# Expert weights in 2-MB tiles with 16-KB runs instead of 1-MB tiles with 8-KB runs

## The chip, the cores and the metric

The kernel runs on one core of a Trainium2 chip. The metric is the device time of one execution in microseconds (us). The engines are called as in the profile: PE (TensorE, matrix products; PEld its weight loads), DVE (VectorE), ACT (ScalarE), POOL (GpSimd) and SP (SyncE, which issues nearly all the DMAs here). One core has 16 DMA engines.

## The reference

Two layers of a diffusion backbone in float32, with 256 tokens of a latent stream and 256 tokens of context, 1024 channels each. Every layer has a front (modulation from a condition vector, layer norm, one wide projection, attention and a gated scan side by side, an output projection, layer norm) and then a mixture of 16 experts:

```python
def expert_choice_ffn(u, w_router, w_gate, w_up, w_down):
    cap = CAPACITY_FACTOR * n // N_EXPERTS            # 32 tokens for each expert
    aff = jax.nn.softmax(u @ w_router, axis=-1)
    top_w, top_idx = lax.top_k(jnp.swapaxes(aff, 1, 2), cap)
    xs = jax.vmap(lambda ub, ib: ub[ib])(u, top_idx)
    h = jax.nn.silu(einsum('becd,edf->becf', xs, w_gate)) * einsum('becd,edf->becf', xs, w_up)
    y = einsum('becf,efd->becd', h, w_down) * top_w[..., None]
    ...                                               # y is added at the chosen tokens

for l in range(2):
    mod = silu(c) @ w_mod[l] + b_mod[l]               # six vectors of 1024: shifts, scales, gates
    ...
    x = post_norm(ALPHA * x + g1 * y, ...)            # y from the token mixer
    u = layer_norm(x) * (1.0 + sc2) + sh2
    x = post_norm(ALPHA * x + g2 * expert_choice_ffn(u, ...), ...)
    ...                                               # layer 0 does the same for the context
```

Each of `w_gate`, `w_up` and `w_down` of an expert is 1024 by 1024 float32, 4 MB. The experts of both layers are 384 MB of the 526 MB that are moved.

## The kernel before, in words

The program is front 0, experts 0, front 1, experts 1. In layer 0 the latent and the context tokens go through the experts together (64 rows for each expert, `S = 2`, `G = 2`), in layer 1 only the latent tokens (32 rows, `S = 1`, `G = 4`). G is the number of column blocks that are computed side by side in PE, NW = 1024 / G is the width of a block and NB = NW / 128.

**The weights.** `moe` walks over the experts e0 to e15. For each, `eload` (L1023) reads gate, up and down as four tiles of 1 MB each. A tile holds 256 rows of the matrix; partition p takes two rows that follow one another in memory, so that a run is 8 KB. SP issues these DMAs at L1029, in the order of the program, through one queue. The last matrix of all, e15's down, is read by `eload_cols` as four tiles of 256 columns (runs of 1 KB), each by two DMAs of 512 KB.

**The slots.** A tile goes into the next slot of a list (`next(slots)`), and the DMA waits until PE has read what stood in that slot. The lists are written by hand at the end of `tile_kernel`, over the slots that `moe_pools` makes: layer 0 has 16 slots for good and two (`once`, tiles `wY` and `wg2 OH`) that serve one time, layer 1 has 19. The list of layer 1 starts with e0's gate in `s[13:17]` and, after 19 MB, comes back to `s[13]`. Since SP issues in order, a DMA that waits for its slot holds up all that are behind it.

**The order of rows.** As partition p holds rows 2p and 2p + 1, product k takes its 128 rows with a step of two: `pairs(v, k)` is the view with that step, and everything that meets the weights along their rows is cut in the same way: the gathered tokens (L1154), `h` before its transposes (L1251), the router weights `wraw` (two DMAs on POOL, L1052) and the modulation of section 6 and 8.

**Modulation.** `mod_steps` computes two of the twelve half-vectors of a layer at a time: it multiplies pieces of `w_mod` (L292), and at the end `mod_cols` (L243) turns the rows into columns by two transposes on PE (L248) and adds the bias on DVE. It does so for q0 = 0 to 10 in steps of two in each layer; q0 = 6 and 8 are the ones whose columns meet the weights.

**Experts on PE.** Gate and up are L1236 (`acc<-w,xs`), down is L1269 (`o<-w,hT`), the end of the last expert L1204 and L1212. A scheduler may move instructions of one engine past one another where data allow it; PE begins the gate of the next expert ahead of the down of this one. A float32 matmul is two records in the trace, a transpose one. Hence 1 MB of weights is 8 records in layer 0 and 16 in layer 1.

Of the kernel before, what the change touches and what calls it, by code (L numbers as in the profile page):

```python
# [19 lines left out]
D = 1024  # L20
# [71 lines left out]

def pairs(v, k):

    return v[:, 256 * (k // 2) + k % 2:256 * (k // 2) + 256:2]

# [11 lines left out]
def tile_kernel(ctx, tc, x, c, ctx_in, c_ctx, w_mod, b_mod, w_in, attn_sink, lb_fw, lb_bw, norm_g,  # L108
# [121 lines left out]
    nc.gpsimd.dma_start(brow, _dram(b_mod, 0, [[256, 48], [1, 256]]))  # L230
    pt = ob()
    for m in range(2):
        nc.tensor.transpose(pt[:, 48 * m:48 * m + 48], brow[:, 128 * m:128 * m + 128], ident[:48, :48])
        nc.tensor.transpose(pt[:, 96 + 48 * m:144 + 48 * m], brow[:, m:256:2], ident[:48, :48])
    for z, a, b in ((0, 0, 6), (1, 6, 10), (0, 10, 12)):
        for m in range(2):
            pv = pt[:, 96 * z + 48 * m:96 * z + 48 * m + 48].rearrange("p (l q j) -> p l q j", l=DEPTH, q=12)
            nc.vector.tensor_copy(BM[:, :, a:b, m::2], pv[:, :, a:b])
    for sec in (1, 4):
        v = BM[:, :, 2 * sec:2 * sec + 2]  # L240
        nc.vector.tensor_scalar(v, v, 1.0, None, op0=ALU.add)

    def mod_cols(l, pm, a, q0, dq, ns):  # L243

        nc.vector.tensor_copy(a, pm[:, 0:256])
        pt = mdb()
        for m in range(2):
            nc.tensor.transpose(pt[:, 128 * m:128 * m + 128], pairs(a, m) if q0 in (6, 8) else a[:, 128 * m:128 * m + 128], ident)  # L248
# [768 lines left out]
    def moe(l, X, M, slots):  # L1017
# [5 lines left out]
        def eload(src, e):  # L1023

            ts = []
            for h in range(4):
                w = next(slots)()
                w = w.rearrange("p (k n) -> p k n", k=2)
                in_order(loads, nc.sync.dma_start(w, _dram(src, (l * NE + e) * D * FF + 256 * h * FF, [[2 * FF, 128], [FF, 2], [1, FF]])))  # L1029
                ts.append(w)  # L1030
            return ts

        def eload_cols(src, e):

            ts = []
            for h in range(4):
                w = next(slots)().rearrange("p (k n) -> p k n", k=KT)
                for i in range(2):
                    in_order(loads, nc.sync.dma_start(w[:, i::2], _dram(src, (l * NE + e) * D * FF + i * FF + 256 * h,
                                                                        [[2 * FF, 128], [256 * FF, KT // 2], [1, 256]])))  # L1040
                ts.append(w)
            return ts

        def wrow(ts, k):
            return ts[k // 2][:, k % 2]

# [3 lines left out]
        nc.gpsimd.memset(wraw, 0.0)  # L1050
        for i in range(2):
            nc.gpsimd.dma_start(wraw[:, i::2, 0:NE], _dram(w_router, l * D * NE + i * NE, [[2 * NE, 128], [256 * NE, KT // 2], [1, NE]]))  # L1052

# [12 lines left out]
        def route(s):  # L1066
# [5 lines left out]
            for i in range(2):  # L1072
# [74 lines left out]
        def gather(gi, s, after=()):  # L1147

            for k4 in range(0, KT, 4):
                p = tr3() if gi else (ob, acc)[k4 // 4]()  # L1150
                for k in range(k4, k4 + 4):
                    for i in range(2):
                        t = 2 * s + i
                        ins = mm(p[:, 128 * (k - k4):128 * (k - k4) + 128], pairs(xh[:, t, :], k),  # L1154
                                 OHs[gi % 2][:, t].rearrange("p e c -> p (e c)"), start=(i == 0), stop=(i == 1))
                        if after:
                            in_order(list(after), ins)
# [68 lines left out]
        for gi in range(4):  # L1226
            for e4 in range(4):
# [38 lines left out]
                for kt in range(KT):  # L1266
                    j, m = kt // NB, kt % NB
                    for dj in range(G):
                        mm(py[MW * dj:MW * dj + MW, :NW], hT[:, 128 * m + MW * j:128 * m + MW * j + MW],  # L1269
                           wrow(wd, kt)[:, NW * dj:NW * dj + NW], start=(kt == 0), stop=(kt == KT - 1))  # L1270
                if e == 0:
# [70 lines left out]
    def moe_pools(l, st, S, zones, right=()):  # L1342

        M, slots, once = {}, [], []
        shapes = {"xh": [2 * S, D], "OH": [2 * S, 4, CAP], "xs": [KT, 4, 32 * S], "oT": [S, 256], **({"OH": [2, 4, CAP]} if S == 1 else {}), "pad": [1024]}
        rest = {"g2": [D], "OH": [2 * S, 4, CAP], "Y": [S, D]}
        parts = []
        for z, names in enumerate((right,) + zones if right else zones):
            Z = pool(sZ, f"ZR{l}", side="right") if names is right else pool(st, f"Z{l}{z}")
            for n in names:  # L1350
                if isinstance(n, int):
                    for i in range(n):

                        w = 2304 if z == 2 + (right != ()) else 2048
                        slots.append(lambda Z=Z, i=i, w=w: Z.tile([128, w], F32, name=f"w{i}", tag=f"w{i}")[:, :2048])
                elif n not in shapes:

                    once.append(lambda Z=Z, n=n: Z.tile([128, 2048], F32, name="w" + n, tag=n))
                    parts.append((n, lambda Z=Z, n=n: Z.tile([128, 2048], F32, name=n, tag=n)))
# [68 lines left out]
```

## Time and profile before

| | |
|---|---|
| median of 3 runs | 1807.12 us (1805.68 to 1808.17) |
| profiled execution, own time | 1810.56 us |
| its span in the profile | 1808.8 us |
| PE busy | 1552.1 us (86% of the span) |
| moved by DMA | 525.93 MB, mean 291 GB/s |
| experts 0, stretch in which DMA is full | about 567 to 960 us |
| experts 1, stretch in which DMA is full | about 1358 to 1777 us |

The own time of the profiled execution is 1.8 us above its span. [...] "x" is a count of records.

### The profile page before, as it was taken

How to read it: one execution, taken by the hardware profiler on the slowest of the kernel's cores; microseconds unless marked ns; L12 is line 12 of the kernel's file. 1: busy time of each engine (PE TensorE's matmuls, PEld its weight loads, DVE VectorE, ACT ScalarE, POOL GpSimd, SP SyncE). 2: the span in 40 equal slices, each digit the busy share in tenths (PEclk: the TensorE clock that was granted, in tenths of full speed). 3: DMA queues.
4: the chain of work that ended last, by engine and by line, in shares of the span. 5: the costliest groups of instructions: out<-in, count | busy, mean ns of one | idle time of the engine just before them, and what ended most of it. 6: DMA issues, size and time to landing. Idle time of an engine off the chain costs nothing.

```text
span 1808.8 us, 27428 instructions
## 1 busy us (share of the span) xinstructions
PE 1552.1 (86%) x11342; PEld 926.5 (51%) x11342; DVE 689.3 (38%) x1458; ACT 468.9 (26%) x884; POOL 296.9 (16%) x298
## 2 busy tenths in 40 slices
PE   6999998999979999898987999998968766766675
PEld 4777775788744433332223788775845322322222
DVE  4656666423651221211213756766751100100102
ACT  2437666423120100001001533676410000000000
POOL 2332222224300000000002633231610000000001
PEclk9999998999989999999999999998969777876877
DMA  9633224524679999999999753422689999999997
GB/s 319 199 105 118 82 71 151 197 85 146 264 301 381 421 421 421 421 422 421 421 422 363 235 159 112 146 94 85 243 337 413 420 421 421 420 421 421 421 421 289
DMA packets 159436, 525.93 MB, mean 291 GB/s; under 512 B 9896, under 2 KB 94064, under 8 KB 111184
## 3 DMA queue, kind: packets, MB, share of 16 engines
q1 hardware_dynamic: 157136, 517.33, 74.1%
q0 software_dynamic: 1456, 4.49, 0.7%
q10 hardware_dynamic: 720, 2.36, 0.4%
q8 instruction: 89, 1.46, 0.3%
q14 instruction: 35, 0.29, 0.0%
HBM read 523.10 MB, written 1.05 MB: 290 GB/s over the span
## 4 chain that ended last, share of the span: by engine, by line
PE 46%; DMA 43%; DVE 4%; ACT 2%; POOL 2%; issue 1%; SPq 1%; POOLq 0%; ACTq 0%; DVEq 0%
DMA w<-in_w_up_dram 14%; DMA w<-in_w_down_dram 14%; DMA w<-in_w_gate_dram 12%; PE acc L166 9%; PE acc L167 8%; PE acc L168 8%; PE acc L1236 5%; PE o L1269 2%; DMA wmod<-in_w_mod_dram 2%; PE md L292 2%; PE sc L740 1%; PE tr L735 1%; PE o L667 1%; PE hs L653 1%; PE sc L716 1%
## 5 line engine op out<-in xcount | busy, mean ns | idle before, releaser
L1236 PE MATMUL acc<-w,xs 128*32 128x256 f32 (+1 forms) x3064 | 406.6, 515 | 95.7 <-DMA w<-in_w_up_dram 51.1
L1236 PEld LDWEIGHTS acc<-w,xs 128*32 128x32 f32 (+1 forms) x3064 | 137.7, 130 | 345.9 <-issue 176.1
L1269 PE MATMUL o<-w,hT 128*32 128x256 f32 (+1 forms) x1432 | 189.3, 513 | 41.2 <-DMA w<-in_w_down_dram 26.8
L166 PE MATMUL acc<-uTh,wh 128*128 128x512 f32 (+1 forms) x592 | 213.1, 361 | 4.7 <-ACT sgs L858 3.6
L167 PE MATMUL acc<-uTl,wh 128*128 128x512 f32 (+1 forms) x592 | 210.2, 355 | 1.1 <-DVE uTl L396 1.1
L168 PE MATMUL acc<-uTh,wl 128*128 128x512 f32 (+1 forms) x592 | 210.1, 355 | 0.0
L1247 ACT ACTIVATE h<-acc 128x512 f32<-128x512 f32 (+1 forms) x32 | 15.7, 491 | 516.5 <-PE acc L1236 503.7
L477 POOL TENSOR_TENSOR wl<-win,wh 128x1024 fp32r<-128x1024 f32 x44 | 111.3, 2531 | 232.5 <-ACT wh L476 230.9
L1269 PEld LDWEIGHTS o<-w,hT 128*32 128x32 f32 (+1 forms) x1432 | 64.4, 132 | 145.5 <-issue 68.2
L1248 DVE TENSOR_TENSOR h<-h,acc 128x512 f32<-128x512 f32 (+1 forms) x32 | 17.7, 552 | 296.0 <-PE acc L1236 296.0
L166 PEld LDWEIGHTS acc<-uTh,wh 128*128 128x128 f32 x592 | 112.2, 190 | 28.7 <-issue 5.1
L167 PEld LDWEIGHTS acc<-uTl,wh 128*128 128x128 f32 x592 | 112.5, 190 | 17.6 <-DVE uTl L396 1.9
L168 PEld LDWEIGHTS acc<-uTh,wl 128*128 128x128 f32 x592 | 112.4, 190 | 15.7 <-issue 1.8
L476 ACT CAST wh<-win 128x1024 fp32r<-128x1024 f32 x84 | 83.9, 1047 | 80.5 <-PE acc L167 48.5
L1128 POOL TENSOR_TENSOR OW<-OH,aff 128x256 f32<-128x256 f32 x8 | 4.9, 617 | 584.5 <-PE sc L1251 569.6
L1292 DVE TENSOR_TENSOR Y<-o,g2 OH 32x512 f32<-32x512 f32 x60 | 41.2, 687 | 137.9 <-PE o L1269 137.1
L477 DVE TENSOR_TENSOR wl<-win,wh 128x1024 fp32r<-128x1024 f32 x40 | 55.5, 1389 | 80.4 <-ACT wh L476 80.4
L1253 ACT COPY hT<-sc 128x512 f32<-128x512 f32 (+1 forms) x32 | 15.3, 479 | 249.0 <-PE sc L1251 248.9
L1292 DVE TENSOR_TENSOR Y g<-o,Y g 32x256 f32<-32x256 f32 x60 | 25.2, 420 | 121.5 <-PE o L1269 120.8
L292 PE MATMUL md<-wmod,scol 128*32 128x256 f32 x640 | 58.0, 422 | 8.0 <-DMA wmod<-in_w_mod_dram 5.3
L562 DVE TENSOR_TENSOR K<-K,F 128x512 f32<-128x512 f32 x56 | 48.1, 859 | 11.0 <-PE hs L634 9.3
L331 POOL TENSOR_TENSOR mv<-mv,nhalf 128x1 f32<-128x1 f32 x26 | 24.4, 941 | 125.8 <-DVE mv L330 125.8
(453 smaller groups left out, 2393.9 us busy)
## 6 DMA issues: line engine op xcount, KB each, us to landing
w<-in_w_gate_dram SPq DMA_DIRECT2D x128, 1024.0 KB, 19.8
w<-in_w_up_dram SPq DMA_DIRECT2D x127, 1024.0 KB, 19.8
w<-in_w_down_dram SPq DMA_DIRECT2D x119, 1024.0 KB, 19.8
wmod<-in_w_mod_dram SPq DMA_DIRECT2D x80, 512.0 KB, 4.6
win<-in_w_in_dram SPq DMA_DIRECT2D x26, 1024.0 KB, 6.2
win<-in_w_in_dram SPq DMA_DIRECT2D x32, 512.0 KB, 5.2
wmod<-in_w_mod_dram SPq DMA_DIRECT2D x32, 256.0 KB, 6.3
wo<-in_w_out_dram SPq DMA_DIRECT2D x8, 1024.0 KB, 5.3
```

The costliest lines, as they stand in the source:

```text
L166: mm(p, a.hi, b.hi, start=start, stop=False, **kw)
L167: mm(p, a.hi, b.lo, start=False, stop=False, **kw)
L168: mm(p, a.lo, b.hi, start=False, stop=stop, **kw)
L292: mm(pm[32 * j:32 * j + 32, 0:256], scol[:, k, :], w[:, 256 * j:256 * j + 256], start=(k == 0), stop=(k == KT - 1))
L331: pows.append(nc.gpsimd.tensor_tensor(mv[:, 2:3], mv[:, 2:3], nhalf[:, 0:1], op=ALU.pow))
L476: nc.scalar.copy(hi[:, r], w[:, r])
L477: ins = eng.tensor_sub(lo[:, r], w[:, r], hi[:, r])
L562: nc.vector.tensor_tensor(kv, kv, _view(f, 0, [[nf + 1, 2], [2, nf // 2], [0, m]]), op=ALU.mult)
L653: mm(p[:, 256 * i:256 * i + 256], K[:, d, 256 + 128 * i:384 + 128 * i], Q[:, d, 0:256], start=(d == 0), stop=(d == 1), skip_group_check=True)
L1236: ins = mm(p[MW * j:MW * j + MW, :NW], xs[:, k, e4, :], wrow(w, k)[:, NW * j:NW * j + NW], start=(k == 0), stop=(k == KT - 1))
L1269: mm(py[MW * dj:MW * dj + MW, :NW], hT[:, 128 * m + MW * j:128 * m + MW * j + MW], wrow(wd, kt)[:, NW * dj:NW * dj + NW], start=(kt == 0), ...
L1292: nc.vector.tensor_tensor(o, py[r:r + 32, :NW], g2[r:r + 32, NW * dj:NW * dj + NW], op=ALU.mult)
```

## The change

The 16 (and 19) MB for weights are cut into 2-MB slots `d` where two neighbours can be taken, 6 in layer 0 and 7 in layer 1, and the slots `s` of 1 MB that are left. A tile in a `d` slot has 512 rows, four consecutive ones on each partition, runs of 16 KB. Where the list says `two`, the same 512 rows go into two 1-MB slots, with runs of 8 KB. Of the 96 steps of 2 MB that a layer takes from its list, 72 are `d` in layer 0 and 71 in layer 1. All that meets the rows is cut with a step of four (`quads`); in layer 1 `h` has two blocks of 128 columns (NB = 2), and so that its transposes still meet the rows, `share` gives gate and up a moving operand of two neighbouring elements in every four. Two transposes in `mod_cols` become eight small products for q0 = 6 and 8 (`fourths`), also once for `b_mod` at the start. The router weights are four DMAs on POOL instead of two, and e15's down four of 256 KB for each MB.

```diff
+    def fourths(o, v, n):
+        for m in range(4):
+            for j in range(2):
+                mm(o[64 * j:64 * j + 64, n * m:n * m + n], v[:, m:256:4], ident[:n, :n], start=True, stop=True, skip_group_check=True)
...
         pt = mdb()
+        if q0 in (6, 8):
+            fourths(pt, a, 128)
...
+                    nc.vector.tensor_tensor(MT[l][r, q0:q0 + 2, :, s], pv[r, :, j, :, s], BM[r, l, q0:q0 + 2, :], op=ALU.add)
+            return
...
         def eload(src, e):
-            for h in range(4):
-                w = next(slots)()
-                w = w.rearrange("p (k n) -> p k n", k=2)
-                in_order(loads, nc.sync.dma_start(w, _dram(src, (l * NE + e) * D * FF + 256 * h * FF, [[2 * FF, 128], [FF, 2], [1, FF]])))
+            for h in range(2):
+                ws = next(slots)()
+                n = 4 // len(ws)
+                for i, w in enumerate(ws):
+                    w = w.rearrange("p (k n) -> p k n", k=n)
+                    in_order(loads, nc.sync.dma_start(w, _dram(src, (l * NE + e) * D * FF + (512 * h + n * i) * FF,
+                                                               [[4 * FF, 128], [FF, n], [1, FF]])))
+                    rows += [w[:, k] for k in range(n)]
...
+        def share(v, j):
+            return v[:, NW * j:NW * j + NW] if NB == 4 else _view(v, 512 * (j // 2) + 2 * (j % 2), [[4, 128], [1, 2]])
...
-        for i in range(2):
-            nc.gpsimd.dma_start(wraw[:, i::2, 0:NE], _dram(w_router, l * D * NE + i * NE, [[2 * NE, 128], [256 * NE, KT // 2], [1, NE]]))
+        for i in range(4):
+            nc.gpsimd.dma_start(wraw[:, i::4, 0:NE], _dram(w_router, l * D * NE + i * NE, [[4 * NE, 128], [512 * NE, KT // 4], [1, NE]]))
...
-                            ins = mm(p[MW * j:MW * j + MW, :NW], xs[:, k, e4, :], wrow(w, k)[:, NW * j:NW * j + NW],
+                            ins = mm(p[MW * j:MW * j + MW, :NW], xs[:, k, e4, :], share(w[k], j),
...
-        a, b, c = s[7:10] + s[13:16], s[10:13], s[0:6]
-        d = a + b[:1] + c[1:6] + b[1:] + c[:1]
-        finish = moe(0, XX, M, itertools.chain(a, once[1:], b, once[:1], c,
-                                               itertools.cycle(d[:WMP] + s[6:7] + d[WMP:])))
+        finish = moe(0, XX, M, itertools.chain(
+            (d[3], d[5], two(s[1], once[1]), d[4], two(s[2], once[0]), d[0], d[1], d[2], two(s[3], s[0])),
+            itertools.cycle((d[3], d[5], d[4], d[1], d[2], two(s[1], s[3]), d[0], two(s[0], s[2])))))
...
-        finish = moe(1, XX, M, itertools.cycle(s[13:17] + s[7:9] + s[17:19] + s[9:13] + s[0:7]))
+        singles = itertools.cycle((s[1], s[2], s[3], s[4], s[0]))
+        a, b = (d[5], d[6], two, two, d[3], d[4], d[0], d[1], d[2]), (two,)
+        finish = moe(1, XX, M, itertools.cycle(a + b + a))
```

**PE in layer 0, where the gate of e1 meets the down of e0.** Before, with `w_4969` to `w_4975` the four tiles of e1's gate, and the tiles on L1269 those of e0's down:

```order
L1236 MATMUL acc<-w_4973,xs 64x512 x4
L1236 MATMUL acc<-w_4975,xs 64x512
L1269 MATMUL o<-w_4858,hT 64x512 x4
L1269 MATMUL o<-w_4860,hT 64x512 x4
L1269 MATMUL o<-wY,hT 64x512 x4
L1269 MATMUL o<-w_4864,hT 64x512 x4
L1236 MATMUL acc<-w_4975,xs 64x512 x3
L1236 MATMUL acc<-w_4977,xs 64x512 x4
```

With the change, `wd_4987` and `wd_4989` being the two tiles of e1's gate:

```order
L1261 MATMUL acc<-wd_4987,xs 64x512 x8
L1261 MATMUL acc<-wd_4989,xs 64x512 x5
L1294 MATMUL o<-ws,hT 64x512 x4
L1294 MATMUL o<-wY,hT 64x512 x4
L1294 MATMUL o<-wd_4882,hT 64x512 x8
L1261 MATMUL acc<-wd_4989,xs 64x512 x3
L1261 MATMUL acc<-ws,xs 64x512 x8
L1261 MATMUL acc<-wd_4995,xs 64x512 x8
```

In both the last three products of e1's gate stand behind the down of e0; what they let go is a slot of 1 MB before, and one of 2 MB after.

**SP in layer 1, the DMAs of e1.** Before, the last row is the first that takes a slot again: that of the first MB of e0's gate.

```order
L1029 DMA w0_10476<-in_w_gate_dram 128x2048 [waits DVE_49,DMAHW4_49,PE_49,Pool_49]
L1029 DMA w1_10478<-in_w_gate_dram 128x2048 [waits DMAHW5_49]
L1029 DMA w2_10480<-in_w_gate_dram 128x2048 [waits DMAHW6_49]
L1029 DMA w3_10482<-in_w_gate_dram 128x2048 [waits DMAHW7_49]
L1029 DMA w0_10484<-in_w_up_dram 128x2048 [waits DMAHW0_49,DVE_49]
L1029 DMA w1_10486<-in_w_up_dram 128x2048 [waits DMAHW1_49]
L1029 DMA w2_10488<-in_w_up_dram 128x2048 [waits DMASW5_49,DMAHW2_49,DMASW4_49,DVE_49]
L1029 DMA w0_10490<-in_w_up_dram 128x2048 [waits DMAHW3_49,PE_49]
```

With the change:

```order
L1049 DMA wd0_10373<-in_w_gate_dram 128x4096 [waits DVE_49,DMAHW1_49,PE_49,Pool_49]
L1049 DMA wd1_10375<-in_w_gate_dram 128x4096 [waits DMAHW2_49]
L1049 DMA wd0_10377<-in_w_up_dram 128x4096 [waits DMAHW3_49,DVE_49]
L1049 DMA ws_10379<-in_w_up_dram 128x2048 [waits DMASW7_49,DMAHW4_49,DMASW6_49,DVE_49]
L1049 DMA ws_10380<-in_w_up_dram 128x2048 [waits DMAHW5_49,PE_49]
L1049 DMA wd0_10383<-in_w_down_dram 128x4096 [waits DMAHW6_49]
```

Here `ws_10380` is the first that takes a slot again, and it is slot `s[1]`, in which the first MB of e0's up stands; 2-MB tiles that could follow into e0's gate slots are queued behind it.

**PE in front 0, the modulation with q0 = 6.** Before, with two transposes between the three products (`wh`, `wl` and the halves of `u`) of a projection:

```order
L735 MATMUL tr<-cst,e 128x128 x4
L167 MATMUL acc<-uTl,wh 128x512
L168 MATMUL acc<-uTh,wl 128x512
L248 MATMUL md<-cst,mrow 128x128 x2
L166 MATMUL acc<-uTh,wh 128x512
```

With the change:

```order
L753 MATMUL tr<-cst,e 128x128 x4
L166 MATMUL acc<-uTl,wh 128x512
L167 MATMUL acc<-uTh,wl 128x512
L235 MATMUL md<-cst,mrow 64x128 x8
L554 MATMUL hs<-Pr,cst 32x128 x4
L165 MATMUL acc<-uTh,wh 128x512
```

The two transposes have become eight matmuls with 64 columns of weights; four small products of the scan (L554) stand in another place too. In front 1 the scheduler has put many rows in another order, for all engines, and on SP the first three loads of `w_in` stand ahead of the `w_mod` loads that they stood behind.

## Rows read from the trace of the kernel before

**Rows 1.** The page: span, and busy time of each engine.
```profile
span 1808.8 us, 27428 instructions
PE 1552.1 (86%) x11342; PEld 926.5 (51%) x11342; DVE 689.3 (38%) x1458; ACT 468.9 (26%) x884; POOL 296.9 (16%) x298
```

**Rows 2.** The page: the chain that ended last, shares of the span by engine.
```profile
PE 46%; DMA 43%; DVE 4%; ACT 2%; POOL 2%; issue 1%; SPq 1%; POOLq 0%; ACTq 0%; DVEq 0%
```

**Rows 3.** Windows: stretches of the two streams, with their columns.
```profile
core 0: us, PE busy (x) PEld busy (x) DVE busy (x) ACT busy (x) POOL busy (x), PEclk, DMA share, GB/s
567.00:960.00 393.00, 363.25 (x1644) 133.34 (x1642) 78.49 (x131) 25.89 (x51) 5.65 (x11) 1.00 1.01 421
1358.00:1777.00 419.00, 290.91 (x3100) 121.19 (x3089) 47.39 (x106) 18.40 (x45) 2.99 (x6) 0.80 1.01 421
```

**Rows 4.** Windows, same columns: loads with 1-KB runs, `w_in` and e15's down.
```profile
985.00:990.00 5.00, 1.10 (x2) 0.30 (x2) 4.90 (x12) 1.99 (x2) 3.20 (x3) 0.84 1.10 348
1782.00:1788.00 6.00, 4.30 (x38) 1.50 (x34) 0.42 (x1) 0.37 (x1) 0.00 (x0) 0.50 1.00 319
```

**Rows 5.** Windows, same columns as Rows 3: the stalls of DMA in either stream.
```profile
558.00:563.00 5.00, 5.00 (x26) 2.32 (x25) 2.74 (x4) 0.60 (x1) 0.00 (x0) 1.00 0.39 125
1350.00:1356.00 6.00, 6.00 (x52) 5.45 (x55) 1.23 (x3) 1.50 (x4) 0.00 (x0) 0.70 0.01 3
```

**Rows 6.** Timeline of PE and SP at these: start, us, engine, line, operation.
```profile
559.34 14.33 PE L1236 MATMUL acc<-w,xs 128*64 128x512 f32 x65
...
562.53 1.76 SPq L1029 DMA_DIRECT2D w<-in_w_up_dram  x4
...
1354.82 7.11 PE L1236 MATMUL acc<-w,xs 128*32 128x256 f32 x128
1355.96 0.33 SPq L1029 DMA_DIRECT2D w<-in_w_up_dram  x1
```

**Rows 7.** Timeline of PE: the last tile of up in layer 0 and layer 1.
```profile
967.82 1.94 PE L1236 MATMUL acc<-w,xs 128*64 128x512 f32 x8 [0.56 <-DMA w<-in_w_up_dram]
1782.86 1.93 PE L1236 MATMUL acc<-w,xs 128*32 128x256 f32 x16 [0.57 <-DMA w<-in_w_up_dram]
```

**Rows 8.** Timeline of DVE and POOL at the start of front 1.
```profile
988.99 2.36 POOL L477 TENSOR_TENSOR wl<-win,wh 128x1024 fp32r<-128x1024 f32 x1 [0.39 <-ACT wh L476]
989.54 0.21 DVE L327 BATCH_NORM_AGGREGATE mv<-st 128x2 f32<-128x12 f32 x1
...
991.30 1.54 POOL L331 TENSOR_TENSOR mv<-mv,nhalf 128x1 f32<-128x1 f32 x1
```

**Rows 9.** Timeline of PE: transposes of the modulation, and small float32 products.
```profile
161.08 1.94 PE L740 MATMUL sc<-eT,va 128*64 128x256 f32 x14
...
211.55 0.40 PE L168 MATMUL acc<-uTh,wl 128*128 128x512 f32 x1
211.79 0.39 PE L248 MATMUL md<-cst,mrow 128*128 128x128 f32 x2
...
212.25 0.39 PE L167 MATMUL acc<-uTl,wh 128*128 128x512 f32 x1
212.48 0.40 PE L168 MATMUL acc<-uTh,wl 128*128 128x512 f32 x1
...
1194.09 0.39 PE L166 MATMUL acc<-uTh,wh 128*128 128x256 f32 x1 [0.36 <-ACT sgs L858]
```

**Rows 10.** Timeline of POOL and DVE: the router weights in layer 1.
```profile
1307.56 1.53 POOL L1052 DMA_DIRECT2D wraw<-in_w_router_dram  x2
1319.67 1.82 POOL L1058 TENSOR_TENSOR oT<-wraw,modT 128x128 f32<-128x128 f32 x2 [8.14 <-DMA wraw<-in_w_router_dram]
1322.06 1.28 DVE L368 SCALAR_TENSOR_TENSOR X<-X,mv,lnp 128x1024 f32<-128x1024 f32 x1 [0.84 <-POOL mv L331]
```

**Rows 11.** Windows, same columns as Rows 3: stretches of front 0 and front 1.
```profile
100.00:200.00 100.00, 100.00 (x829) 77.65 (x829) 62.78 (x146) 58.38 (x112) 29.79 (x28) 1.00 0.35 106
1200.00:1300.00 100.00, 85.50 (x702) 70.05 (x702) 66.22 (x157) 64.39 (x130) 32.13 (x34) 0.90 0.42 143
```

More of the change, by code (lines that the diff above doesn't have):

```diff
@@ L42 @@
 BURST = (1, 5)
-WMP = 12
 AHEAD = (2, 7)
@@ L90, in _view, with quads @@
     return bass.AP(tensor=t.tensor, offset=t.offset + offset, ap=[list(t.ap[0])] + pattern)
[L93 to L95 removed]
+def quads(v, k):
+    return v[:, 512 * (k // 4) + k % 4:512 * (k // 4) + 512:4]
 class HL:
@@ L231, in tile_kernel @@
     pt = ob()
+    def fourths(o, v, n):
+        for m in range(4):
+            for j in range(2):
+                mm(o[64 * j:64 * j + 64, n * m:n * m + n], v[:, m:256:4], ident[:n, :n], start=True, stop=True, skip_group_check=True)
     for m in range(2):
         nc.tensor.transpose(pt[:, 48 * m:48 * m + 48], brow[:, 128 * m:128 * m + 128], ident[:48, :48])
[L234 to L237, printed above, removed]
+    fourths(pt[:, 96:], brow, 48)
+    for m in range(2):
+        pv = pt[:, 48 * m:48 * m + 48].rearrange("p (l q j) -> p l q j", l=DEPTH, q=12)
+        for a, b in ((0, 6), (10, 12)):
             nc.vector.tensor_copy(BM[:, :, a:b, m::2], pv[:, :, a:b])
+    for m in range(4):
+        pv = pt[:, 96 + 48 * m:144 + 48 * m].rearrange("p (l q j) -> p l q j", l=DEPTH, q=12)
+        for j in range(2):
+            r = slice(64 * j, 64 * j + 64)
+            (nc.scalar.copy if j else nc.vector.tensor_copy)(BM[r, :, 6:10, m], pv[r, :, 6:10, j])
     for sec in (1, 4):
@@ L246, in mod_cols @@
         pt = mdb()
+        if q0 in (6, 8):
+            fourths(pt, a, 128)
+            pv = pt.rearrange("p (m q j r) -> p q j m r", m=4, q=2, j=2)
+            for s in range(ns):
+                for j in range(2):
+                    r = slice(64 * j, 64 * j + 64)
+                    nc.vector.tensor_tensor(MT[l][r, q0:q0 + 2, :, s], pv[r, :, j, :, s], BM[r, l, q0:q0 + 2, :], op=ALU.add)
+            return
         for m in range(2):
-            nc.tensor.transpose(pt[:, 128 * m:128 * m + 128], pairs(a, m) if q0 in (6, 8) else a[:, 128 * m:128 * m + 128], ident)
+            nc.tensor.transpose(pt[:, 128 * m:128 * m + 128], a[:, 128 * m:128 * m + 128], ident)
         pv = pt[:, 0:256].rearrange("p (m q j r) -> p q j m r", m=2, q=2, j=2)
@@ L1050, in moe @@
         nc.gpsimd.memset(wraw, 0.0)
-        for i in range(2):
-            nc.gpsimd.dma_start(wraw[:, i::2, 0:NE], _dram(w_router, l * D * NE + i * NE, [[2 * NE, 128], [256 * NE, KT // 2], [1, NE]]))
+        for i in range(4):
+            nc.gpsimd.dma_start(wraw[:, i::4, 0:NE], _dram(w_router, l * D * NE + i * NE, [[4 * NE, 128], [512 * NE, KT // 4], [1, NE]]))
         pl = tr()
@@ L1269, in moe @@
                         mm(py[MW * dj:MW * dj + MW, :NW], hT[:, 128 * m + MW * j:128 * m + MW * j + MW],
-                           wrow(wd, kt)[:, NW * dj:NW * dj + NW], start=(kt == 0), stop=(kt == KT - 1))
+                           wd[kt][:, NW * dj:NW * dj + NW], start=(kt == 0), stop=(kt == KT - 1))
                 if e == 0:
@@ L1342, in moe_pools @@
     def moe_pools(l, st, S, zones, right=()):
-        M, slots, once = {}, [], []
+        M, slots, once = {}, ([], []), []
         shapes = {"xh": [2 * S, D], "OH": [2 * S, 4, CAP], "xs": [KT, 4, 32 * S], "oT": [S, 256], **({"OH": [2, 4, CAP]} if S == 1 else {}), "pad": [1024]}
@@ L1351, in moe_pools @@
                 if isinstance(n, int):
-                    for i in range(n):
+                    for i in range(n // 2):
+                        slots[0].append(lambda Z=Z, i=i: [Z.tile([128, 4096], F32, name=f"wd{i}", tag=f"wd{i}")])
+                    if n % 2:
                         w = 2304 if z == 2 + (right != ()) else 2048
-                        slots.append(lambda Z=Z, i=i, w=w: Z.tile([128, w], F32, name=f"w{i}", tag=f"w{i}")[:, :2048])
+                        slots[1].append(lambda Z=Z, w=w: [Z.tile([128, w], F32, name="ws", tag="ws")[:, :2048]])
                 elif n not in shapes:
-                    once.append(lambda Z=Z, n=n: Z.tile([128, 2048], F32, name="w" + n, tag=n))
+                    once.append(lambda Z=Z, n=n: [Z.tile([128, 2048], F32, name="w" + n, tag=n)])
                     parts.append((n, lambda Z=Z, n=n: Z.tile([128, 2048], F32, name=n, tag=n)))
@@ L1395, in tile_kernel, with two @@
         M, s, once = moe_pools(1, st, 1, ([4], [3], [1], ["xh", "xs", "oT", "OH", "pad", 1], [4], [4], [1], [1], ["Y g2"]))
-        finish = moe(1, XX, M, itertools.cycle(s[13:17] + s[7:9] + s[17:19] + s[9:13] + s[0:7]))
+        d, s = s
+        singles = itertools.cycle((s[1], s[2], s[3], s[4], s[0]))
+        def two():
+            return next(singles)() + next(singles)()
+        a, b = (d[5], d[6], two, two, d[3], d[4], d[0], d[1], d[2]), (two,)
+        finish = moe(1, XX, M, itertools.cycle(a + b + a))
         finish()
```

29 lines of the change are left out of this document (16 added, 13 removed).

## The prediction

> **What bounds the kernel now.** PE is busy for 86% of the span and DMA moves all through two long stretches, so I first read who ends last: the chain that ended last is 46% PE and 43% DMA, and no other engine has more than 4% [rows 1, 2]. The windows say where each rules. From 567 to 960 us and from 1358 to 1777 us the DMA engines are full (share 1.01) at 421 GB/s, while PE works for 363.25 of 393 us in layer 0 and for 290.91 of 419 us in layer 1, there at a mean granted clock of 0.80 [rows 3]. These are the expert streams: 1 MB takes 1048576 / 421e9 = 2.49 us, whatever PE does. Between the streams PE or the chain through it rules: front 0 has PE busy for 100.00 of 100 us, front 1 for 85.50 of 100 [rows 11]. So the change is worth what it does to four things: the rate of the stream, how many MB a stream holds when it starts for good, what PE has to do once the last tile has landed, and what the fronts carry.
>
> **The rate.** What one run of 16 KB takes no row shows; two runs of other lengths bound it. At 421 GB/s over 16 engines a run of 8 KB takes 8192 x 16 / 421e9 = 311.3 ns [rows 3]. Where loads have runs of 1 KB, the same full engines move 348 GB/s (the `w_in` loads), or 47.1 ns a run [rows 4]. A straight line through the two has a fixed part of 47.1 - (311.3 - 47.1) / 7 = 9.3 ns for each run, so that 16 KB would take 613.3 ns where two of 8 KB take 622.6. A 2-MB tile is 128 runs, 8 for each engine: 8 x 9.3 = 0.0746 us saved. It counts only while DMA is full: of layer 0's 72 tiles of 2 MB about 10 are loaded ahead and one is read by columns, 61 stay; of layer 1's 71, 7 are loaded ahead and 2 read by columns, 62 stay. 123 x 0.0746 = **-9.2 us**. Bounds: 0, if the fixed part does not belong to a run but to 8 KB or less; and -14.0 with the other row of 1-KB runs (319 GB/s, 51.4 ns, fixed part 14.2 ns) [rows 4]. I take the first row, whose stretch has no late landing in it, as the end of a kernel's last load has.
>
> [...]
>
> **Where the streams start for good.** In layer 0 DMA stops near 558 us: in the five microseconds from there its share is 0.39 [rows 5]. PE has begun e1's gate ahead of e0's down, and the last quarter of it stands behind that down, as the order shows for before and after alike; SP goes on at 562.53 [rows 6]. What has been let go by then is another amount. Before: 17 MB of first use, 7 MB from e0's gate and up (the eighth stood in a slot of one use), and 3 MB of e1's gate, 27. After: 18 of first use, 6 (`d3`, `d5`, `d4`) and the first 2 MB of e1's gate, 26. The place at which PE lets go is the same, so 1 MB more is left to load at 421 GB/s: **+2.5 us** (bounds: 0, if PE, which the full stream leaves 30 us, makes it good later, and 5.0, if the step behind waits too and a second MB is missing).
>
> In layer 1 DMA has filled all 19 MB and stands still until PE begins the experts (share 0.01) [rows 5]. Before, the first slot to come back is that of e0's first MB; PE starts at 1354.82, does 8 MB of gate and up in 7.11 us (128 records, 16 for each MB), that is 0.89 us each, and SP issues at 1355.96 [rows 6]. After, the first slot that comes back is that of the first MB of up, after 5 MB of products; all later DMAs are queued behind it on SP. The stream starts 4 x 0.89 = **+3.6 us** later. This lies on the path, for nothing but the stream decides the next 419 us.
>
> [...]
>
> **The fronts.** Each `fourths` is 8 float32 products, 16 records with 128 columns; 64-wide ones of 256 columns take 1.94 / 14 = 0.139 us, half of that is 0.069, together 1.1 us. The two transposes that go cost 0.23: the four rows from 211.55 to 212.48 take 0.93 us, of which three steps of 0.233 are the products' own [rows 9]. That makes +0.88 at four places, PE being full in front 0 [rows 11], less the 0.36 us that PE waits for ACT behind one of them in layer 1 [rows 9]: **+3.1** (bounds 0, if they fill gaps, and 8.0, if a record costs 0.139 whatever its columns). The `fourths` of `b_mod` stand where PE waits for the first `w_mod` loads: 0, or 1 us without that cover.
>
> In front 1, POOL computes a `wl` for 2.36 us ahead of the power on `mv`, whose input is there at 989.75 and which starts at 991.30 [rows 8]; with `w_in` issued ahead of `w_mod` that `wl` is over earlier: **-1.5** (bound 0, if the next `wl` takes its place). The router weights in layer 1: two DMA issues on POOL take 1.53 us, POOL idles 8.14 us until they have landed, and DVE then 0.84 us on POOL [rows 10]. Two more issues are 1.5 us, of which DVE's wait lets most through: **+1.0** (0 to 1.5). The gapped operand of `share`, the step of four in `h` and the gathers are 0: they run on a PE with 128 us to spare in layer 1's stream [rows 3].
>
> **Sum.** -9.2 + 2.5 + 3.6 + 1.8 + 1.9 + 3.1 - 1.5 + 1.0 = +3.2 us. The profiled execution's own time is 1810.56 us (span 1808.8 and 1.8 around it), 3.4 above the median of the runs; it would become 1813.8, and the median 1807.12 + 3.2 = **1810.3 us**. 0.2% of the time is 3.6 us, about what a measurement of this kernel tells from no change.
>
> **Rivals.**
> - *Runs of 16 KB are no faster.* If a transfer costs by the byte from 8 KB on, the saving is 0 and the costs stay: +12.4, **1819.5 us**, slower. For it: 421 GB/s in both streams although one has a busy PE and the other does not, as at a ceiling [rows 3]. Against: the line through 1 and 8 KB has a slope of 16 x 1024 / 37.7 ns = 434 GB/s, so 421 is not its end. It decides from 12.4 / 123 = 0.10 us for a tile, or 12.6 ns for a run: below that the change costs time. [...]
> - *The fronts gain from their new order.* The scheduler has put front 1's rows on PE in another order. PE idles 14.5 us in the 100 us from 1200 [rows 11]; half of it saved is 7 us, **1803.3**, faster. Or the saving for a run is the 14.2 ns of the other row and the `fourths` and router loads are hidden: 1807.12 - 14.0 + 2.5 + 3.6 + 1.8 + 1.9 - 1.5 = **1801.4**.
> - *The new order loses as much:* the same 7 us with the other sign, **1817.3**, slower.
> - *The gapped operand runs at half rate in layer 1.* Then the 5 MB before the stream starts take 4.4 us more and the last 2 MB of up 3.9 more: **1818.6**. Gate and up would also fill most of PE's 128 spare us. No row shows a product with such an operand.
>
> **Chances.** The sum as it stands, to within 0.2% of before: 0.42. No faster runs: 0.14. Fronts gain 0.14, larger saving 0.13: faster together 0.27. Fronts lose 0.11, gapped operand 0.06: with the first rival, slower 0.31. The range of 1800.5 to 1819 us leaves out half of the largest saving and the upper half of the slow cases, about 0.2; the main case's own range is 1804 to 1814, its costs of streams (0 to +9.8) and fronts going partly against each other.
>
> **What the profile would show.** In the two streams about 425 GB/s where 421 stood (three quarters of the bytes at 427), and 16-KB tiles among the issues; 421 would show the rate wrong. The first SP issue after layer 1's fill about 4.7 us after PE begins the experts instead of 1.1; the DMA share near 558 us lower for longer. PE's row after the last up tile with 16 and 32 records, near 3.7 us. L235 at about 1.1 us each, four times; a longer POOL wait for `wraw`. The prediction is wrong if the fronts, which no term but the last three touches, differ in length by more than 5 us, or if the stream's rate moves by less than 1 GB/s or more than 7.

## The result, and the profile after

The changed kernel takes 1833.22 us (1831.11 to 1833.63) where the kernel before takes 1807.64: a ratio of 1.0138 (95% interval 1.0126 to 1.0150), 25.6 us slower. Its profiled execution has a span of 1831.2 us, 22.4 more than before [rows 1]; the profiled execution of the kernel before, 1810.56 us, was 2.9 us slower than that kernel's median. One execution of ten, in the experiment on the order of layer 1 with packed tokens, took 2538.02 us at a mean granted clock of 0.553 of full speed and is left out of that experiment's median.

The stages are read from the timelines of PE, as the start of the first product of each:

| first product of | before, us | after, us | later by |
|---|---|---|---|
| router, layer 0 | 489.10 | 492.27 | 3.2 |
| gather ahead of e0 | 519.00 | 520.85 | 1.9 |
| e0's gate, layer 0 | 530.01 | 538.37 | 8.4 |
| e15's down, layer 0 | 972.10 | 988.89 | 16.8 |
| router, layer 1 | 1331.25 | 1352.09 | 20.8 |
| e0's gate, layer 1 | 1354.82 | 1377.16 | 22.3 |
| e15's down, layer 1 | 1786.62 | 1809.01 | 22.4 |

Layer 1's stream, for which the prediction had the largest terms, costs 0.1 us. The loss is in four other places: front 0 (3), the few microseconds of the gather ahead of e0 (5), layer 0's stream (8) and front 1 (4, and 1.5 in its gather).

The first thing that the windows show is that the rate came as forecast: in the middle of either stream of the changed kernel DMA moves 426 GB/s, where rows 3 had 421 (columns as there, PEclk being the granted clock of TensorE as a share of full speed):

```profile
620.00:940.00 320.00, 299.37 (x1296) 122.73 (x1294) 64.54 (x109) 22.83 (x46) 3.08 (x5) 0.99 1.01 426
1400.00:1770.00 370.00, 243.13 (x2593) 119.24 (x2596) 42.79 (x95) 15.33 (x38) 2.99 (x6) 0.82 1.01 426
```

But PE no longer waits for it in layer 0. These are the groups of PE's instructions from 530 to 990 us in the kernel before (line, operation, shape, count, busy us, mean ns of one, idle time before them and who ended it):

```profile
L1236 PE MATMUL acc<-w,xs 128*64 128x512 f32 x1016 | 231.5, 597 | 7.6 <-DMA w<-in_w_up_dram 5.3 <-DMA w<-in_w_gate_dram 2.2
L1269 PE MATMUL o<-w,hT 128*64 128x512 f32 x472 | 109.3, 597 | 8.8 <-ACT hT L1253 8.0 <-DMA w<-in_w_down_dram 0.7
L1251 PE MATMUL sc<-cst,h 128*128 128x128 f32 x64 | 11.6, 304 | 11.1 <-DVE h L1248 11.1
...
L1154 PE MATMUL hs<-g2 OH,xh 128*128 128x128 f32 x48 | 6.9, 290 | 0.6 <-DVE xs L381 0.6
L1154 PE MATMUL tr<-g2 OH,xh 128*128 128x128 f32 x48 | 6.6, 288 | 0.0
```

and in the changed one:

```profile
L1261 PE MATMUL acc<-wd,xs 128*64 128x512 f32 x784 | 177.8, 597 | 0.0
...
L1261 PE MATMUL acc<-ws,xs 128*64 128x512 f32 x232 | 54.3, 594 | 0.0
...
L1179 PE MATMUL tr<-g2 OH,xh 128*128 128x128 f32 x48 | 12.5, 408 | 0.0
L1179 PE MATMUL hs<-g2 OH,xh 128*128 128x128 f32 x48 | 12.0, 408 | 0.6 <-DVE xs L399 0.6
```

Gate and up waited 7.6 us for DMA before and wait 0.0 now, and the gather (L1154, now L1179) takes PE nearly twice as long: its six groups with 192 records there sum to 26.9 us before and 48.4 us after. What became slower is the load of the weights. The list of the gather's line gives minimum, median and maximum in ns; in the kernel before:

```profile
L1154 PEld LDWEIGHTS md<-OH,xh x64: 193/196/197, 651.4 to 1566.5; 128*128 128x128 f32 x64
L1154 PE MATMUL md<-OH,xh x64: 281/281/386, 651.4 to 1566.6; 128*128 128x128 f32 x64
```

and in the changed one:

```profile
L1179 PEld LDWEIGHTS md<-OH,xh x64: 307/329/332, 662.7 to 1585.3; 128*128 128x128 f32 x64
L1179 PE MATMUL md<-OH,xh x64: 273/397/500, 662.7 to 1585.5; 128*128 128x128 f32 x64
```

The tokens `xh` are the weights of this product (the operand of its LDWEIGHTS records, whose time changes with the step of `xh`), and their 128 columns stand 8 bytes apart with `pairs` and 16 with `quads`. These medians are at full clock (granted 1.00). Ahead of e0 a part of the gather runs at a granted clock of 0.50, and there the step costs little: the load takes 331 ns before and 329 after. In the kernel before, the first row here is at 0.50 and the second at 1.00:

```profile
519.00 3.63 PE L1154 MATMUL o<-OH,xh 128*128 128x128 f32 x16
528.03 2.05 PE L1154 MATMUL acc<-OH,xh 128*128 128x128 f32 x16
```

and so they are in the changed one:

```profile
520.85 4.10 PE L1179 MATMUL o<-OH,xh 128*128 128x128 f32 x16 [0.71 <-DVE OH L1145]
534.54 3.90 PE L1179 MATMUL acc<-OH,xh 128*128 128x128 f32 x16
```

From the start of one record to that of the next this is 118 ns before and 233 after at full clock, and 213 and 233 at half (medians). With the step of four a record begins every 233 ns at either clock.

The end of layer 0's stream shows who is late. PE's timeline there:

```profile
971.65 1.02 PE L1219 MATMUL sc<-Y,oT 96*128 96x512 f32 x2
972.60 13.95 PE L1261 MATMUL acc<-wd,xs 128*64 128x512 f32 x64
987.41 0.75 PE L1276 MATMUL sc<-cst,h 128*128 128x128 f32 x4 [0.86 <-DVE h L1273]
```

All 8 MB of e15's gate and up go through in one piece with no wait for a load, where before each of the last three tiles was waited for (0.37, 0.57 and 0.56 us; rows 7 has the last).

What was forecast for layer 1 can be read too. SP and PE at its start:

```profile
1377.16 3.83 PE L1261 MATMUL acc<-wd,xs 128*32 128x256 f32 x64
1380.82 3.81 PE L1261 MATMUL acc<-ws,xs 128*32 128x256 f32 x64
...
1381.96 0.33 SPq L1049 DMA_DIRECT2D ws<-in_w_up_dram  x1
1382.34 0.90 SPq L1049 DMA_DIRECT2D wd<-in_w_down_dram  x2
```

SP goes on 4.80 us after PE begins the experts, where it was 1.14 [rows 6]: 3.7 us later. The last tile of up, and one `fourths`:

```profile
1804.12 3.24 PE L1261 MATMUL acc<-wd,xs 128*32 128x256 f32 x32 [1.86 <-DMA wd<-in_w_up_dram]
```

```profile
1160.96 1.23 PE L235 MATMUL md<-cst,mrow 128*64 128x128 f32 x16
```

The tail is 3.24 us where it was 1.93 [rows 7], and 16 records of the small products take 1.23 us (estimated: 1.1).

### The profile page after: what moved, and what is told of

It is laid out like the page before. It is cut to its first block, busy times and chain, and to the rows that moved or that the text cites. A ratio compares the mean times of both kernels' runs of the same rounds, so it can differ in the third digit from the quotient of the medians.

```text
span 1831.2 us, 27282 instructions
## 1 busy us (share of the span) xinstructions
PE 1574.0 (86%) x11412; PEld 983.1 (54%) x11412; DVE 688.5 (38%) x1460; ACT 466.1 (25%) x886; POOL 297.3 (16%) x302
## 5 line engine op out<-in xcount | busy, mean ns | idle before, releaser
L1261 PE MATMUL acc<-wd,xs 128*32 128x256 f32 (+1 forms) x2320 | 302.0, 513 | 68.0 <-DMA wd<-in_w_up_dram 40.2
L1261 PEld LDWEIGHTS acc<-wd,xs 128*32 128x32 f32 (+1 forms) x2320 | 112.2, 130 | 242.7 <-issue 166.4
L1294 PE MATMUL o<-wd,hT 128*32 128x256 f32 (+1 forms) x1024 | 136.4, 525 | 34.4 <-DMA wd<-in_w_down_dram 29.0
L1294 PEld LDWEIGHTS o<-wd,hT 128*32 128x32 f32 (+1 forms) x1024 | 51.5, 135 | 106.5 <-issue 66.6
L1261 PE MATMUL acc<-ws,xs 128*32 128x256 f32 (+1 forms) x744 | 91.4, 472 | 12.5 <-DMA ws<-in_w_gate_dram 8.4
L1261 PEld LDWEIGHTS acc<-ws,xs 128*32 128x32 f32 (+1 forms) x744 | 33.2, 121 | 63.9 <-issue 39.3
## 6 DMA issues: line engine op xcount, KB each, us to landing
wd<-in_w_up_dram SPq DMA_DIRECT2D x47, 2048.0 KB, 21.5
```

Of the source, the lines that this page charges most:

```text
L1261: ins = mm(p[MW * j:MW * j + MW, :NW], xs[:, k, e4, :], share(w[k], j), start=(k == 0), stop=(k == KT - 1))
```

## The experiments

Theory A: the gather's weight load pays for the step of four, and this turns PE into the bound of layer 0's stream. Rival B: layer 0 loses by the new order of slots and the larger tiles, and the gather only costs what stands ahead of e0. Times are medians; the kernel before is at 1807.3 to 1807.7 us beside all of them, and ratios are to it. Lengths of stages are those of one profiled execution.

**The step alone, taken from the changed kernel and put into the one before.**

```diff
-ins = mm(p[...], quads(xh[:, t, :], k), ...)
+ins = mm(p[...], xh[:, t, 256 * (k // 2) + k % 2:256 * (k // 2) + 256:2], ...)
```

> The changed kernel, with only the gather's view of the tokens (L1179) back at a step of two; its columns then meet the wrong rows of the weights, so the output is not the reference's; every engine has the same instructions in the same order. Theory A (the weight load of a product slows down when its 128 columns stand 16 bytes apart: 329 ns against 196 ns in the traces; this costs 5.2 us before e0 in layer 0, 1.5 us in layer 1, and makes PE the bound of layer 0's stream): the time falls by 14 to 16 us, to about 1818 us, and the products of the gather take 281 ns again. Theory B (the loss of layer 0's stream comes from the new order of slots and the larger tiles; the gather only costs what stands ahead of e0): it falls by 6.7 us at most, to about 1826.5 us.

1815.80 us, ratio 1.0045 (1.0029 to 1.0062), 17.4 us less than the changed kernel. The load is at 196 ns again (median), PE waits for DMA again in layer 0, and e15's down begins at 971.64 us, 0.5 before the kernel before:

```profile
L1179 PEld LDWEIGHTS md<-OH,xh x64: 193/196/197, 647.7 to 1564.1; 128*128 128x128 f32 x64
```

```profile
L1261 PE MATMUL acc<-wd,xs 128*64 128x512 f32 x784 | 178.2, 596 | 10.7 <-DMA wd<-in_w_up_dram 7.9 <-DMA wd<-in_w_gate_dram 2.7
```

The same edit the other way round (`pairs` to a step of four) in the kernel before:

> The kernel before, with only the gather's view of the tokens (L1154) at a step of four; its columns then meet the wrong rows of the weights, so the output is not the reference's; the order of all engines is as before. Theory A (strided weight load): 64 records ahead of e0 and 32 in layer 1 cost 6 to 8 us, and the other 192 of layer 0 put about 23 us more on a PE that has some 25 us of idle there, so a few more: 1807.6 plus 8 to 15, 1816 to 1822 us. Theory B (slots and tiles): only the first part, 1813.5 to 1815.5 us, with layer 0's stream as long as before.

1826.76 us, ratio 1.0103 (1.0088 to 1.0118), 19 us slower, with the old tiles and slots. Its groups of PE from 530 to 990 us:

```profile
L1236 PE MATMUL acc<-w,xs 128*64 128x512 f32 x1016 | 228.2, 595 | 0.0
...
L1154 PE MATMUL hs<-g2 OH,xh 128*128 128x128 f32 x48 | 12.4, 405 | 0.6 <-DVE xs L381 0.6
```

From e0's gate to e15's down layer 0 takes 453.6 us in it, 442.1 before: 11.5 us. The gather ahead of e0 takes 5.0 us more, and that of layer 1 1.5. B falls. A stands, at more than its numbers: the two runs gave 1.4 and 4 us more than the upper end that it had.

**The length of a run.** Each 2-MB tile by two DMAs:

```diff
+for r in range(0, n, 2):
+    dma_start(w[:, r:r + 2], ... (512 * h + n * i + r) * FF, [[4 * FF, 128], [FF, 2], [1, FF]])
```

> The changed kernel with each 2-MB tile loaded by two DMAs, each of two rows per partition (runs of 8 KB), into the same slots. Theory A (a run has a fixed part of about 9 ns, so that 16 KB move at 425 to 426 GB/s where 8 KB move at 421): the streams fall back to 421 GB/s; layer 1, which DMA bounds, loses 4 to 5 us; layer 0, which PE bounds now, loses 0 to 2: about 1838 us. Theory B (the length of a run beyond 8 KB does nothing; the higher rate has another cause): 425 to 426 GB/s stay, and the time stays within 2 us of 1833.

1836.98 us, ratio 1.0160 (1.0144 to 1.0176), 3.8 us more than the changed kernel, with 421 GB/s in either stream; layer 1's stream (e0's gate to e15's down) is 434.8 us long, 431.9 in the changed kernel: 2.9 us, less than the 4 to 5 of A. The rate falls back as A has it; the 3.8 us are little more than the two intervals leave open. The edit changes two things, the length of a run and the size of a DMA (1 MB instead of 2). In the trace of the changed kernel both are under way from 620 to 940 us, 8-KB runs in DMAs of 1 MB and 16-KB runs in DMAs of 2 MB: there a packet of 8 KB takes 313 ns (median of 4123) and one of 16 KB 614 ns (median of 6259), 12 ns less than two of 8 KB. No run has the one without the other.

**The small products.** Two transposes in their place:

```diff
-if q0 in (6, 8):
-    fourths(pt, a, 128)
...
+nc.tensor.transpose(pt[...], a[:, m:256:2] if q0 in (6, 8) else a[:, 128 * m:128 * m + 128], ident)
```

> The changed kernel with the two transposes back in place of the eight small products, in the modulation of q0 = 6 and 8 and for the bias at the start (the columns of these sections are then in the order of before and meet the wrong rows, so the output is not the reference's). Theory A (front 1 loses 4 to 4.5 us by its new order on PE, whatever causes that order): front 0 gives back the 3.2 us that it is longer, front 1 little: about 1830 us. Theory B (the small products also hold up front 1): about 1825.5 us.

1820.37 us, ratio 1.0073 (1.0056 to 1.0089), 12.9 us less: more than either theory. Front 0 gives back about 4 us, front 1 (e15's down to e0's gate) is 384.3 us long where it was 388.3, and layer 0's stream is 3.3 us shorter, with PE still its bound: the scheduler has put PE's rows there in another order too. The products alone, in the kernel before:

> The kernel before with the small products in place of the two transposes, in the modulation of q0 = 6 and 8 and for the bias at the start (these columns are then in the order of the change and meet the wrong rows, so the output is not the reference's). Theory A (16 records take 1.23 us where two transposes took 0.23, four times, and 1 us at the start): 1807.7 + 4 to 5, about 1812 us. Theory B (the products also bring the scheduler to another order, which costs front 1 another 2 us or more, and the start of front 0): 1815 to 1818 us. Theory C (they fill gaps): 1808 us.

1812.84 us, ratio 1.0032 (1.0020 to 1.0045): 5.5 us, nearest to A. In its profiled execution e0 begins 3.0 us late and front 1 loses nothing (380.0 us, 382.7 before). So the products are worth 5 to 6 us in this kernel. Front 1 is 380.0 to 382.7 us long in the four traces of kernels made from the one before (this one among them), 385.9 to 388.3 in four of changed ones with the products, 383.4 to 385.7 in four with transposes in their place, and 380.1 to 381.1 in the two with gapped products of `w_mod` below. So it follows neither the tiles nor the products alone. That points to the order of its instructions, but no run shows it by itself.

**Versions that compute the reference.** In the first the layer norm writes the tokens so that a product's columns lie side by side:

```diff
+dst = dst.rearrange("p (g m r) -> p g m r", m=pack, r=128)
+src = src.rearrange("p (g r m) -> p g r m" , m=pack, r=128)      # iterated as g, m, r
```

> The changed kernel; the layer norm that writes the tokens for the router and the gather now reads its source with a step of four and writes so that the 128 columns of a product lie side by side; the computation is the reference's. Theory A (the weight load pays for the step; side by side it takes about 140 ns, as for the identity at L266): the gather is as fast as with a step of two or faster, and the time is that of the run with a step of two or up to 3 us less, 1812 to 1816 us. Rival: DVE and ACT pay for the strided read in the layer norm, on the path ahead of the router, 1 to 2 us in each layer: 1817 to 1820 us.

1817.55 us, ratio 1.0065 (1.0050 to 1.0080). The load takes 192 ns (186 to 192), not the 140 expected: side by side is no better than 8 bytes apart, and the theory's "or up to 3 us less" fails. The 1.8 us more than with a step of two are within what front 0 differs between executions (it ends 486 to 489 us after the start in two kernels with its instructions unchanged), but they also lie in the rival's range, and its mechanism is in the trace. The layer norm's read with a step of four takes ACT 2.27 us instead of 1.24, and DVE 1.20 instead of 0.80, and later PE waits 1.1 us longer for ACT's tokens. The changed kernel, then this run:

```profile
485.85 1.24 ACT L361 ACTIVATE xh<-X,mr,mv 128x1024 f32<-128x1024 f32 x1 [24.83 <-PE acc L166]
503.91 1.23 PE L1104 MATMUL sc<-cst,xh 128*128 128x128 f32 x8 [0.81 <-ACT xh L361]
```

```profile
487.57 2.27 ACT L364 ACTIVATE xh<-X,mr,mv 128x1024 f32<-128x1024 f32 x1 [24.83 <-PE acc L166]
506.56 1.97 PE L1107 MATMUL sc<-cst,xh 128*128 128x128 f32 x8 [1.91 <-ACT xh L364]
```

The two versions that follow pay this too. The second takes the small products out as well:

```diff
+v = _view(w, 512 * (j // 2) + 2 * (j % 2), [[4, 128], [1, 2]])   # moving operand for q0 = 6, 8
+nc.gpsimd.dma_start(BM[:, l, 6:10], _dram(b_mod, (12 * l + 6) * 512, [[4, 128], [512, 4], [1, 4]]))
```

> The run before this one in this list, and in addition no small products: for q0 = 6 and 8 the products of w_mod take a moving operand of two neighbouring elements in every four, so that two transposes suffice, and the bias of these sections is loaded in its place by two DMAs on POOL; the computation is the reference's. Theory A (the small products cost what the run with transposes in their place gained, 13 us with the step-four gather, of which some 4 us in front 0 and 4 us in front 1 are theirs alone): 6 to 9 us faster than the packed run, about 1806 us. Rival (a gapped moving operand slows down a product): 256 records at L310 become longer by up to their 0.12 us, up to 30 us slower, and layer 1's gate and up (0.0594 us a record against 0.0556) would be only the start of it.

1808.35 us, ratio 1.0007 (0.9997 to 1.0016): the change's loss is gone. The products of `w_mod` are hardly longer (median 387 ns where it was 379, mean of the line 414 where it was 413 in the changed kernel), so the rival falls. The third starts layer 1 in the slots that come back first:

```diff
-a, b = (d[5], d[6], two, two, d[3], d[4], d[0], d[1], d[2]), (two,)
+a, b = (two, d[5], d[6], two, d[3], d[4], d[0], d[1], d[2]), (two,)
...
+c = 2 if (src is w_up and e == 15 and h) else n                  # that half by two DMAs
```

> The run before this one in this list, and in addition in layer 1 the first 2 MB of e0 go into the two 1-MB slots that come back first, so that SP goes on after 1 MB of products instead of 5, and the second half of e15's up is read by two DMAs. Theory A (layer 1's stream starts 3.6 us late in the changed kernel, and the last 2-MB tile adds 1.8 to 1.9 us to either end): 3.6 us plus 2 to 4 us less than the run without, about 1801 us. Rival (the slots that come first now are free later in front 1, and e0 waits for them): same or slower than the run without.

1808.80 us, ratio 0.9999 (0.9987 to 1.0011): by the medians nothing, against A. The profiled execution, in which PE begins the experts at 1352.26, is the fastest of the nine, which spread from 1803.85 to 1811.20; layer 1's stream is 427.8 us long in it, where it is 431.2 in the run without. Its rows on SP show that the edit does less than A has it do:

```profile
1353.44 0.33 SPq L1039 DMA_DIRECT2D ws<-in_w_up_dram  x1
1354.35 4.86 SPq L1039 DMA_DIRECT2D ws<-in_w_down_dram  x2
```

Two DMAs of 1 MB go out 1.2 and 2.1 us after PE begins. The third, the second of the last row, goes out at 1358.88, after 6.6 us, for its slot holds the third MB of up; in the changed kernel SP goes on after 4.8 us with one DMA upon the other. So the slots move 2 MB forward and not the stream. The rival, that e0 waits for its slots, is not shown. The kernel before with its tokens side by side:

> The kernel before with its tokens written so that the 128 columns of a product lie side by side (pairs there); the computation is the reference's. Theory A (a step of two costs the weight load 196 instead of 140 ns): the gather ahead of e0 in either layer gains 1 to 2 us, layer 0's stream nothing, since DMA bounds it: 1804 to 1807 us. Rival (a step of two costs nothing, only a step of four does): 1807 us as before, or 1 us more for the layer norm.

1808.00 us, ratio 1.0002 (0.9993 to 1.0012), load 192 ns: the rival holds, a step of two costs nothing that the time shows.

**What is left of the tiles themselves.** Both losses undone, tiles and slots as changed:

> The changed kernel with both undone: the gather at a step of two and the two transposes in place of the small products (columns then meet the wrong rows, so the output is not the reference's); the 2-MB tiles, the slots and the 16-KB runs stay. Theory A (what is left of the change is what the prediction summed for the streams: -9.2 for the rate, +2.5 and +3.6 for their starts, +3.7 for the last tiles, and about nothing in the fronts): 1807.7 - 9.2 + 9.8, about 1808 us. Theory B (the gains of the two runs add up: -17.4 and -12.9 from 1833.2): 1803 us.

1806.31 us, ratio 0.9995 (0.9986 to 1.0003): nearer to A's 1808 than to B's 1803, and no change that can be told from none. Its streams are 0.8 us (layer 0) and 1.1 us (layer 1) shorter than before. With the order of layer 1 and the split last tile:

> The run before this one in this list with layer 1's first 2 MB in the two 1-MB slots that come back first, and the second half of e15's up by two DMAs (output as there). Theory A (SP goes on 3.6 us earlier in layer 1, and the tails lose their 1.8 and 1.9): 4 to 7 us less than the run before it. Theory B (as the medians of the runs with packed tokens seemed to say, these starts and ends do not decide): within 1.5 us of it.

1804.92 us, ratio 0.9993 (0.9982 to 1.0004): 1.4 us less than the run before it. Layer 1's stream is 1.7 us shorter, and SP stands again as in the run with packed tokens (from 1.2 and 2.1 to 6.6 us after PE begins). The time is B's, and a gain over the kernel before is not shown. And with runs of 8 KB:

> The first run of this list with each 2-MB tile read by two DMAs with runs of 8 KB (output as there), so that now DMA bounds both streams. Theory A (16-KB runs save 0.0746 us a tile, 123 tiles): 8 to 10 us more than the first run of this list, and 421 GB/s in either stream. Theory B (the end of a stream hides part of it: two DMAs let PE begin after half a tile): 4 to 6 us more.

1814.17 us, ratio 1.0042 (1.0030 to 1.0054), 7.9 us more than with runs of 16 KB: just under the 8 to 10 of A, with its 421 GB/s, and above the 4 to 6 of B. The windows of this run, and then of the one with 16 KB:

```profile
620.00:940.00 320.00, 292.36 (x1293) 103.94 (x1294) 63.64 (x105) 20.21 (x40) 4.42 (x9) 0.99 1.01 421
1400.00:1770.00 370.00, 245.87 (x2506) 95.05 (x2498) 40.68 (x90) 14.95 (x37) 2.37 (x5) 0.79 1.01 421
```

```profile
620.00:940.00 320.00, 288.91 (x1293) 105.64 (x1293) 64.27 (x105) 19.43 (x39) 4.42 (x9) 0.99 1.01 426
1400.00:1770.00 370.00, 227.13 (x2527) 102.55 (x2517) 41.94 (x93) 14.59 (x36) 2.37 (x5) 0.84 1.01 425
```

What is loaded differs in the length of the runs and the size of the DMAs, and the rate goes with the two: 421 GB/s in either stream with 8 KB and 1 MB, 426 and 425 with 16 KB and 2 MB.

## Why the prediction was wrong

**The step that failed** is the sentence by which "the step of four in `h` and the gathers are 0: they run on a PE with 128 us to spare in layer 1's stream". It gave the gathers cover and no price: it never asked what the step does to the load of the weights, and for cover it looked at layer 1. Three quarters of layer 0's gather (192 of 256 records) lie in layer 0's stream, where rows 3 left PE 30 of 393 us. From 530 to 990 us PE waited 19 us for `h` and `hT` (L1251 and L1269 in the rows above), and the longer gather did not fill these waits: in the kernel before with a step of four they are 11.1 and 8.0 us as before. The 21.5 us more of gather made PE the bound there. And 64 records of layer 0 and 32 of layer 1 stand ahead of e0, on the path. By the run in the kernel before, this step was worth 19 us instead of 0. No row of the prediction prices such a load, so nothing held this term at 0. The prediction's own sign of being wrong came with it: up to e0 of layer 0 the changed kernel is 8.4 us late, more than the 5 us that it named for the fronts.

What the step does to a load stands in the traces. The gather's load takes 192 ns with its float32 columns side by side, 196 ns with them 8 bytes apart and 329 ns with them 16 apart, at full clock, and the layer norm's reads on ACT go the same way: 1.24 us side by side, 1.35 at 8 bytes and 2.27 at 16. Not every load does: that of the router's transposes, with the same tokens, takes 209 ns at 8 and at 16 bytes, and 140 side by side. Why 16 bytes cost so much more than 8 no run shows.

**Point by point.**
- *Rate, -9.2:* right. 421 became 426 GB/s, and 8 KB instead of 16 cost 7.9 us where DMA bounds both streams. With three quarters of the bytes in 2-MB tiles, 426 is 427.7 for these (0.75 / x + 0.25 / 421 = 1 / 426), or 613 ns for a run of 16 KB, as the line through 1 and 8 KB gave; the packets show 614. In the changed kernel it was worth less than half, 3.8 us, since PE bound layer 0.
- *Starts of the streams, +2.5 and +3.6:* of the second the delay is seen (SP 3.7 us later), its price is not: the two runs with other first slots gained 1.4 us or nothing by their medians, and they moved only 2 MB. The first can't be read apart.
- *Ends, +1.8 and +1.9:* no run shows either of them as a term by itself. What the traces show in their place is a tail of layer 1 that is 1.3 us longer, 3.24 us instead of 1.93. In layer 0 PE was late anyway and waited for no load: its last 64 records of gate and up take 13.95 us in one piece.
- *Sum of the streams,* -0.3 and +0.9 by these terms: with the two losses undone -0.8 and -1.1 were measured. In layer 1 that is a gain where a loss was forecast, so that the total of the streams came near is in part luck.
- *Small products, +3.1:* 1.23 us for 16 records instead of 1.1, and the kernel with them alone 5.5 us. What was set at 0, those for the bias at the start, adds little: in the kernel with them alone PE's first product of q0 = 4 begins at 54.03 us instead of 53.65. With 4.0 us for the four places, about 1 us stays open.
- *Router weights, +1.0:* not seen. The first product of the router's bias is 20.8 us late in layer 1, as are PE's products ahead of it. POOL's issues take 2.85 us instead of 1.53, but POOL then waits 7.23 us for them instead of 8.14 [rows 10].
- *Start of front 1, -1.5:* 0.5, from 16.8 to 16.3 us late at its first projection. Over the whole of it front 1 lost 4 us, a little over half of what the rival "the new order loses as much" gave; that the order does it is argued and not shown.
- *The gapped operand of `share`:* 128 records take 7.39 us from the first start to that of the next product (1377.16 to 1384.55), 7.05 before (1354.82 to 1361.87): 5% and not half rate, at full clock in both, 0.2 us up to SP's DMA. That rival fell.

Gather 19, small products 5.5, tiles and slots -1.0 (the three runs that have one each) sum to 23.5 of the 25.6 us. The rest is open: it would have to come from what these do to one another, and the order of front 1 is the likeliest place. No run changed that order by itself.

## What to carry to other kernels

When the layout of a loaded matrix changes, list every operand that must follow it, and for each ask on which side of PE it stands: here the new layout cost a moving operand 2 to 5% (387 ns instead of 379, 7.39 us instead of 7.05) and a transpose no more than the old one (283 ns with either), but as weights it cost two thirds more for each load (329 ns instead of 196). An engine that reads with the step can pay too, as ACT did in the layer norm (2.27 us instead of 1.24). Take the cover of a term from the stage in which its instructions stand: layer 1 had 128 us to spare and layer 0 had 30. A gain of the DMA rate pays in a stream only as long as the same edit leaves DMA its bound: here the higher rate was worth 7.9 us where DMA bounded both streams, and 3.8 us where PE bounded layer 0's.

## What the runs showed of the hardware that was not expected

- The load of 128 float32 columns of weights takes 192 ns side by side, 196 ns at 8 bytes apart and 329 ns at 16, at full clock; the product behind it goes from 281 to 397 ns. At a granted clock of 0.50 it takes 331 ns at 8 bytes and 329 at 16.
- As the source of a transpose the same tokens cost no more with a step of four than with two: the router's transposes take 283 ns in either kernel at full clock (273 with the tokens side by side). A moving operand of two elements in every four costs little: 387 ns instead of 379 at `w_mod`, 5% at gate and up of layer 1.
- ACT reads 1024 float32 in 1.24 us side by side and in 2.27 with a step of 16 bytes, DVE in 0.80 and 1.20; with a step of 8 bytes they take 1.35 and 0.81.
- With three quarters of the bytes in 2-MB tiles with runs of 16 KB DMA moves 426 GB/s, and 421 with all of them in runs of 8 KB, its 16 engines full in either (share 1.01). That makes about 428 for the 2-MB tiles alone, an estimate from the two rates. A packet of 16 KB takes 614 ns, one of 8 KB 313.
